# A two-layer hybrid decoder trunk on one core: the first k tile of x^T is multiplied with the first three weight blocks ahead of the second k tile

## The chip, the core and the metric

The kernel runs on one core of a Trainium2 chip. The metric is device time in microseconds (us) of one execution; lower is better. A core has a matrix engine (TensorE, PE in the profile; its weight loads are the row PEld), VectorE (DVE), ScalarE (ACT), GpSimd (POOL) and SyncE (SP), which here only issues transfers (DMAs) to the core's 16 DMA engines. Each engine works through its own instructions in order and waits at semaphores for the others.

## What is computed

Two layers, each with an RMS norm, one wide input projection, four groups of heads, a gate for each group, an output projection and a residual, and a last RMS norm:

```
def hybrid_layer(x, layer_idx, norm_g, w_in, ..., w_out, rope_diff, rope_moba):
    h = rms_norm(x, norm_g)
    p = split_columns(jnp.einsum("bsd,de->bse", h, w_in))
    ...
    mixed = jnp.concatenate([fox, diff, moba, gla], axis=-1)
    return x + jnp.einsum("bse,ed->bsd", mixed, w_out)
```

x is 256 x 2048 in fp32 and w_in has 2048 rows for each layer. Only the start of the first layer's input projection matters in what follows.

## The kernel before

**Three products for one.** The projections are done in a reduced form of fp32 (fp32r), and every operand is split into a high and a low part: `hi` is the operand rounded to fp32r, and `lo` the rest. A product takes three matmuls, high times high, low of x times high of the weights, and high of x times low of the weights. ScalarE makes the high part of the weights (`hi_of`, line 730), VectorE the low part (`lo_of`, line 733). Both are bound to a helper that records each operation, so nearly all instructions show line 466 in the profile, and one goes by the tiles' names.

**x^T.** The transposed x stands ready in memory (`in_xt`) and is loaded into tiles `four`, four k tiles of 128 rows to a tile. `xt_hi` (line 1561) scales a k tile with the norm's weights (`ngt`) into the high half of `hTp`, and `xt_lo` (line 1568) makes the low half on VectorE. The high half is made on VectorE for k tile 0 and on ScalarE for all others. The norm's row factor comes later, from the squares of x^T, and is applied to the results.

**Blocks and steps.** The columns of w_in are cut into blocks. A step is one block with two k tiles (four for a narrow block): one load into a tile `raw` (of which there are 5), a split into `hi` and `lo` (4 of each), then 12 matmuls, since x has two halves of 128 rows (m = 0, 1), 2 k tiles and 3 products. The results of a block add up in PSUM in `mm` tiles or, for the third block, in a `side` tile. In each layer the first three blocks, here A (348 columns), B (512) and C (348), take turns: A, B, C with k tiles 0 and 1, then with k tiles 2 and 3, and so on.

**The first three steps** (`HALVED = 3`) are loaded and split by halves, one k tile each. A0 is block A with k tile 0, A1 with k tile 1, and likewise B0, B1, C0 and C1. The transfers of SyncE are issued by `load` (line 1540), in the order A0, x^T tile 0, A1, x^T tile 1, B0, B1, x^T tiles 2 and 3, C0, C1. The splits are written by `parts_of` (line 1609), step by step: both halves of A with the two x^T tiles, then both halves of B, then of C. `multiply` (line 1812) sorts the products of such a step by half, so TensorE has A0, A1, B0, B1, C0, C1.

**What sets the order of the rest.** A planner in the program (`fill`, `choose`, `split_for`) keeps a rough clock of its own and places each later split and transfer by it when the program is built. A new load into a `raw` tile waits until the split of the step that had the tile is done. The order on each engine is fixed in the built program.

Before the first weights arrive, TensorE multiplies constants (`keep_warm`, line 665).

Of the kernel before, what the change touches and what calls it, by code (L numbers as in the profile page):

```python
# [21 lines left out]
P = 128  # L22
# [15 lines left out]
HALVED = 3  # L38
# [332 lines left out]
def hybrid_trunk(  # L371
# [17 lines left out]
    nc = tc.nc  # L389
    times = Times()  # L390
    cur = {"task": None}

    def give(op):
        if cur["task"] is None:
            emit(op)
        else:
            cur["task"].fifo.append(op)
# [70 lines left out]
    def given_out(key):  # L468
        give(Op("do", lambda: ready.__setitem__(key, times.last)))
# [30 lines left out]
    def fill():  # L500

        for z in list(added):
            if z[0] <= times.now + SOON:
                added.remove(z)
                z[1]()
        load_more()
        busy = True
        while busy:
            busy = False
            passive()  # L510
            for kind in "av":
                e = engines[kind]
                while e.tail < times.now + HORIZON and choose(kind, e):
                    busy = True
                    passive()
# [51 lines left out]
    def matmul(out, lhsT, rhs, start, stop, tiles=1, main=False, **kw):  # L567
        n = int(np.prod(rhs.shape[1:]))
        us = (n * 4 if lhsT.dtype == F32 else n + 32) / 2400.0 / tiles
        give(Op("t", partial(t_.matmul, out, lhsT, rhs, start=start, stop=stop, **kw), [rhs] if main else [lhsT, rhs],  # L570
                [] if main else [out], us))
        if main:
            times.end(out, times.now, "t")
# [156 lines left out]
    def hi_of(hi, src, scale=1.0):  # L730
        a_.activation(hi, src, AF.Copy, scale=scale)

    def lo_of(lo, src, hi):
        v_.tensor_sub(lo, src, hi.bitcast(F32))
# [741 lines left out]
    plan = []  # L1476
# [5 lines left out]
        b = blocks[z["block"]]  # L1482
        plan.append({**z, "block": b, "need": {(b["need"], b["l"], k // 4) for k in z["kts"]}})

    xts = []
    ys = xs.rearrange("p m d -> p (m d)").rearrange("p (c j n) -> p c j n", c=4, j=2)
    mTf = [t.rearrange("p k s -> p (k s)").rearrange("p (f k s) -> p f k s", f=4, k=8) for t in mT]
    orders, ys_to_load, y_free, y_at = [], deque(), {}, {}
# [7 lines left out]
    loads = {"next": 0, "out": 0, "freed": deque(), "at": 0, "left": 0.0, "open": 0}  # L1496

    def load_x(eng, a, b):
        if a % 4 == 0:
            xts.append(s4.get([P, 4, SEQ]))  # L1500
        eng.dma_start(xts[a // 4][:, a % 4:(b - 1) % 4 + 1], xt[:, a:b])
# [38 lines left out]
    def load(i):  # L1540
        s = plan[i]
        if i == 0:
            nc.scalar.dma_start(ngt, norm_gt)
        if i < 24 and i % 6 == 0 and i:
            load_x(nc.sync, i // 6 * 4, i // 6 * 4 + 4)
        per, n = s["block"]["per"], s["block"]["n"]
        raw = wst.tile([P, STEP_W], F32, name="raw", bufs=RAW_BUFS)
        raw = raw[:, :per * n]
        s["raw"] = raw.rearrange("p (j c) -> p j c", j=per)
        src = weights[s["at"]:s["at"] + P * per * n].rearrange("(p c) -> p c", p=P)  # L1550
        if i < HALVED:
            for j in range(2):
                nc.sync.dma_start(raw[:, j * n:(j + 1) * n], src[:, j * n:(j + 1) * n])
                if i == 0:
                    load_x(nc.sync, j, j + 1)
        else:
            q_.move(raw, src, LOADED)
        if i == 1:
            load_x(nc.sync, 2, 4)

    def xt_hi(kt):
        src, g = xts[kt // 4][:, kt % 4], ngt[:, 0, kt:kt + 1]
        if kt == 0:
            v_.tensor_scalar(hT[0][:, kt], src, g, None, op0=OP.mult)
        else:
            hi_of(hT[0][:, kt], src, g)

    def xt_lo(kt):
        v_.scalar_tensor_tensor(hT[1][:, kt], xts[kt // 4][:, kt % 4], ngt[:, 0, kt:kt + 1], hT[0][:, kt].bitcast(F32),
                                op0=OP.mult, op1=OP.subtract)  # L1570

    def split_xt(kts):

        for kt in kts:
            xt_hi(kt)
        for kt in kts:
            xt_lo(kt)
        if kts[-1] % 4 == 3:
            given_out(("h", 0, kts[-1] // 4))
# [29 lines left out]
    def parts_of(s):  # L1609
        per, n = s["block"]["per"], s["block"]["n"]  # L1610
        for name in ("hi", "lo"):
            if s["block"]["kind"] == "apart":
                s[name] = s4.get([P, per, n], F32R)
                continue
            t = wst.tile([P, PART_W], F32R, name=name, bufs=PART_BUFS)
            s[name] = t[:, :per * n].rearrange("p (j c) -> p j c", j=per)
        if not any(s is z for z in plan[:HALVED]):
            s["stages"] = deque([("a", lambda: hi_of(s["hi"], s["raw"]), lambda: times.of(s["raw"])),
                                 ("v", lambda: lo_of(s["lo"], s["raw"], s["hi"]), lambda: times.of(s["hi"]))])
            return  # L1620
        for j in (slice(0, 1), slice(1, 2)):
            hi_of(s["hi"][:, j], s["raw"][:, j])
            if s is plan[0]:
                split_xt((j.start,))
            lo_of(s["lo"][:, j], s["raw"][:, j], s["hi"][:, j])
        loads["freed"].append(times.of(s["lo"]))

    def sum_forms(l):

# [116 lines left out]
    def open_parts(i):  # L1746
        (form_parts if "pair" in plan[i] else parts_of)(plan[i])
# [64 lines left out]
    def multiply(s):  # L1812
        b = s["block"]
        n, (lh, ll) = b["n"], b["lhs"]
        ps = b["ps"]
        if b["kind"] == "apart":
            b.setdefault("steps", []).append(s)
            if s["last"]:
                b["ps1"] = side.get([P, 1024])
            for m, o, steps in ((0, ps[0], [s]), (1, b.get("ps1"), b["steps"])):  # L1820
                if m == 1 and not s["last"]:
                    break
                for z in steps:
                    for j, kt in enumerate(z["kts"]):
                        first, last = z["first"] and j == 0, z["last"] and j == len(z["kts"]) - 1
                        hi, lo, ts = z["hi"][:, j], z["lo"][:, j], slice(m * P, (m + 1) * P)
                        matmul(o[:, :n], lh[:, kt, ts], hi, first, False, main=True)
                        matmul(o[:, :n], lh[:, kt, ts], lo, False, False, main=True)
                        matmul(o[:, :n], ll[:, kt, ts], hi, False, last, main=True)
            return  # L1830
        order = list(enumerate(s["kts"]))
        end = s["last"], len(order) - 1
        products = [(x, part, j, kt) for x, part in ((lh, "hi"), (ll, "hi"), (lh, "lo")) for j, kt in order]
        if any(s is z for z in plan[:HALVED]):
            products.sort(key=lambda z: z[2])
        products = [(*z, m) for z in products for m in range(2)]
        if (s["first"] or s["last"]) and not any(s is z for z in plan[:HALVED]):
            products.sort(key=lambda z: z[4])
        for k, (x, part, j, kt, m) in enumerate(products):
            if k and k % 6 == 0:  # L1840
                loads["left"] = lasts(s) * (1 - k / len(products))
                fill()
            matmul(ps[m][:, :n], x[:, kt, m * P:(m + 1) * P], s[part][:, j],
                   s["first"] and j == 0 and x is lh and part == "hi", part == "lo" and (True, j) == end, main=True)
# [32 lines left out]
    def take_bank(keep=True):  # L1877
        k = banks["next"].popleft()
        if keep:
            banks["next"].append(k)  # L1880
        settle(waiting, k)
        return k, mm.tile([P, 512], F32, name=f"mm{k}", bufs=1)

    def lasts(z):
        return 1.36 if "pair" in z else len(z["kts"]) * (z["block"]["n"] + 32) / 400.0
# [7 lines left out]
    for i in range(ahead):  # L1893
        prepare(i)
        parts_of(plan[i])
        plan[i]["stages"] = ()
# [10 lines left out]
    for i, s in enumerate(plan):  # L1907
# [10 lines left out]
        if i in x_at:  # L1918
            l, k = x_at[i]
            c = slice(k * 512, k * 512 + 512)  # L1920
            src = kept.rearrange("p (m d) -> p m d", m=2)[:, :, c] if l else x[0, :, c].rearrange("(m p) c -> p m c", p=P)
# [5 lines left out]
        if "pair" in s:  # L1927
            if s["form"] == FORM_ORDER[0] and s["first"]:
                k, ps = take_bank(False)
# [58 lines left out]
```

## Time and profile before

| | |
|---|---|
| median of 3 runs | 893.13 us (893.09, 893.13, 894.57) |
| the profiled execution | 892.94 us |
| its span, first to last instruction | 891.2 us |
| TensorE busy | 881.5 us, 99% of the span |
| VectorE, ScalarE busy | 662.2 us, 559.1 us |
| mean granted TensorE clock | 0.998 |
| moved by DMA | 227.45 MB, 255 GB/s in the mean |

A row of the timeline gives the start, the length, the engine, the line, the operation with its output and inputs, their shapes, a count where like instructions follow each other, and in brackets the idle time ahead of it and what ended that. ACTq and SPq are the instruction queues of ScalarE and SyncE, where DMAs are issued. In the list of DMAs the last figure of a row is the time from issue to landing. The chain of waits is followed back from the last instruction of the stretch that was asked for.

### The profile page before, as it was taken

Reading aid. Unit: us, or ns where it says so; the run is one execution under the profiler, and the core shown is the slowest. Engines: PE = TensorE matmul, PEld = TensorE weight load, DVE = VectorE, ACT = ScalarE, POOL = GpSimd, SP = SyncE. Lnnn points to the kernel's source line nnn. Section 1 sums busy time; section 2 is a strip of 40 time slices with the busy share of each in tenths; the row PEclk is TensorE's granted clock in tenths of the full one; section 3 lists DMA queues with packets and bytes.
Section 4 is the critical chain, followed back from the end, with each engine's and each line's share of the span. In section 5 each row is a group of like instructions: output and inputs, shape, how many; then the busy total and the mean of one; then the engine's idle time right before and its main releaser. Section 6 shows DMA issues by size and latency. Waiting matters only on the chain.

```text
span 891.2 us, 12456 instructions
## 1 busy us (share of the span) xinstructions
PE 881.5 (99%) x4380; PEld 750.8 (84%) x4380; DVE 662.2 (74%) x943; ACT 559.1 (63%) x846; POOL 60.0 (7%) x87
## 2 busy tenths in 40 slices
PE   9999999999999999999999999999999999999996
PEld 7988889888887888888899888898888888888886
DVE  6689878878867967656679778879676788585583
ACT  7577675577646667644756876578644575693461
POOL 1010110000110000000000100110000100101000
PEclk9999999999999999999999999999999999999999
DMA  8889897747988685977798898878958978499742
GB/s 289 294 263 303 266 301 241 254 147 263 288 240 274 203 317 178 362 265 228 235 302 265 285 320 224 253 227 277 337 147 262 301 220 271 168 301 363 236 143 96
DMA packets 84142, 227.45 MB, mean 255 GB/s; under 512 B 9979, under 2 KB 30443, under 8 KB 83950
## 3 DMA queue, kind: packets, MB, share of 16 engines
q1 hardware_dynamic: 73336, 192.00, 63.9%
q0 software_dynamic: 9152, 33.03, 14.5%
q10 hardware_dynamic: 1590, 1.62, 0.5%
q8 instruction: 34, 0.56, 0.3%
q14 instruction: 30, 0.25, 0.1%
HBM read 204.06 MB, written 22.55 MB: 254 GB/s over the span
## 4 chain that ended last, share of the span: by engine, by line
PE 93%; DVE 2%; DMA 2%; issue 1%; ACT 1%; SPq 0%; POOLq 0%; POOL 0%; DVEq 0%; ACTq 0%
PE mm L466 79%; PE side L466 14%; DMA raw<-in_weights 2%; DVE lo L466 1%; DVE four L466 1%; ACT hi L466 1%; DMA far<-four 0%; DVE mTl L466 0%; ACT four L466 0%; ACT L466 0%; DVE raw L466 0%; DVE eight L466 0%; SPq L466 0%; POOLq L1984 0%; POOL rf L466 0%
## 5 line engine op out<-in xcount | busy, mean ns | idle before, releaser
L466 ACT ACTIVATE hi<-raw 128x1024 fp32r<-128x1024 f32 (+2 forms) x319 | 316.6, 1011 | 190.9 <-PE mm L466 110.2
L466 PE MATMUL mm<-hi,hTp 128*128 128x512 f32 (+1 forms) x1760 | 432.7, 381 | 1.2 <-ACT hTp L466 0.9
L466 DVE TENSOR_TENSOR lo<-raw,hi 128x1024 fp32r<-128x1024 f32 (+2 forms) x319 | 363.7, 1157 | 93.3 <-ACT hi L466 89.0
L466 PEld LDWEIGHTS mm<-hi,hTp 128*128 128x128 f32 x1760 | 321.5, 188 | 60.3 <-ACT hi L466 1.3
L466 PE MATMUL mm<-lo,hTp 128*128 128x512 f32 (+1 forms) x880 | 237.4, 380 | 0.1
L466 PEld LDWEIGHTS mm<-lo,hTp 128*128 128x128 f32 x880 | 162.4, 188 | 30.6 <-DVE lo L466 0.8
L466 PE MATMUL mm<-hi,mTh 128*128 128x512 f32 (+1 forms) x256 | 69.3, 377 | 0.0
L466 PE MATMUL mm<-lo,mTh 128*128 128x512 f32 (+1 forms) x256 | 69.0, 376 | 0.1
L466 PE MATMUL mm<-hi,mTl 128*128 128x512 f32 (+1 forms) x256 | 69.0, 376 | 0.0
L466 PEld LDWEIGHTS mm<-lo,mTh 128*128 128x128 f32 x256 | 46.2, 188 | 9.2 <-DVE lo L466 0.5
L466 PEld LDWEIGHTS mm<-hi,mTl 128*128 128x128 f32 x256 | 46.3, 188 | 8.8
L466 PEld LDWEIGHTS mm<-hi,mTh 128*128 128x128 f32 x256 | 46.0, 188 | 8.6 <-ACT hi L466 0.4
L466 ACT ACTIVATE four<-mm,rstd 128x512 f32<-128x512 f32 (+2 forms) x56 | 36.7, 667 | 26.3 <-PE mm L466 26.3
L466 POOL DMA_DIRECT2D four<-far x40 | 21.8, 546 | 444.0 <-DMA far<-four 193.5
L466 DVE STREAM_TRANSPOSE four<-four 128x1024 f32<-128x1024 f32 (+1 forms) x34 | 39.1, 1149 | 6.7 <-ACT four L466 6.3
L466 ACT ACTIVATE four<-four 128x512 fp32r<-128x512 f32 (+3 forms) x44 | 35.5, 819 | 12.6 <-DMA four<-far 8.8
L466 PEld LDWEIGHTS side<-four,four 128*128 128x128 f32 (+1 forms) x336 | 37.7, 190 | 3.9 <-issue 1.8
L466 PE MATMUL side<-four,four 128*128 128x128 f32 (+3 forms) x336 | 39.3, 281 | 0.0
L1686 POOL DMA_DIRECT2D xs<-in_weights x24 | 21.2, 900 | 169.5 <-DVE lo L466 36.2
L466 DVE TENSOR_TENSOR lo<-xs,hi 128x1024 fp32r<-128x1024 f32 x24 | 29.1, 1214 | 1.8 <-ACT hi L466 1.8
L466 ACT ACTIVATE mTh<-four 128x1024 fp32r<-128x1024 f32 x16 | 16.9, 1057 | 21.2 <-DVE four L466 21.1
L466 ACT ACTIVATE hi<-xs 128x1024 fp32r<-128x1024 f32 x24 | 25.4, 1060 | 7.1 <-PE mm L466 6.2
(146 smaller groups left out, 685.1 us busy)
## 6 DMA issues: line engine op xcount, KB each, us to landing
raw<-in_weights SPq DMA_DIRECT2D x271, 512.0 KB, 4.9
four<-far POOLq DMA_DIRECT2D x34, 512.0 KB, 6.7
far<-four SPq DMA_DIRECT2D x128, 128.0 KB, 3.9
raw<-in_weights SPq DMA_DIRECT2D x46, 348.0 KB, 5.1
xs<-in_weights POOLq DMA_DIRECT2D x24, 512.0 KB, 8.5
xs<-in_weights SPq DMA_DIRECT2D x8, 512.0 KB, 8.3
xs<-in_x SPq DMA_DIRECT2D x4, 512.0 KB
kept<-xs SPq DMA_DIRECT2D x1, 2048.0 KB, 10.6
```

Of the source, the lines that this page charges most:

```text
L466: op.do()
L1686: g_.eng.dma_start(ys[:, c], weights[at:at + P * 1024].rearrange("(p j c) -> p j c", p=P, j=2), accum_op=OP.add)
```

## The change

The first three steps are still loaded, split and multiplied by halves, but the outer loop now runs over the halves: all of A0, B0, C0 stands ahead of A1, B1, C1, in the transfers, in the splits and in the matmuls. The high part of x^T's k tile 1 is made by VectorE, as that of k tile 0 is. x^T tiles 2 and 3 are loaded after the six halves. The rest of the program is the same but for the planner's order in the steps that follow at once; from the fourth group of x^T's k tiles on, all engines have the same order in both.

```diff
     def load(i):
 ...
         if i < HALVED:
-            for j in range(2):
-                nc.sync.dma_start(raw[:, j * n:(j + 1) * n], src[:, j * n:(j + 1) * n])
-                if i == 0:
-                    load_x(nc.sync, j, j + 1)
+            firsts.append((raw, src, n))
+            if i + 1 == HALVED:
+                for j in range(2):
+                    for k, (to, part, m) in enumerate(firsts):
+                        nc.sync.dma_start(to[:, j * m:(j + 1) * m], part[:, j * m:(j + 1) * m])
+                        if not k:
+                            load_x(nc.sync, j, j + 1)
+                load_x(nc.sync, 2, 4)
         else:
             q_.move(raw, src, LOADED)
-        if i == 1:
-            load_x(nc.sync, 2, 4)
 
     def xt_hi(kt):
         src, g = xts[kt // 4][:, kt % 4], ngt[:, 0, kt:kt + 1]
-        if kt == 0:
+        if kt < 2:
             v_.tensor_scalar(hT[0][:, kt], src, g, None, op0=OP.mult)
         else:
             hi_of(hT[0][:, kt], src, g)
 ...
-        for j in (slice(0, 1), slice(1, 2)):
-            hi_of(s["hi"][:, j], s["raw"][:, j])
-            if s is plan[0]:
-                split_xt((j.start,))
-            lo_of(s["lo"][:, j], s["raw"][:, j], s["hi"][:, j])
-        loads["freed"].append(times.of(s["lo"]))
+        if s is plan[HALVED - 1]:
+            for j in range(2):
+                for z in plan[:HALVED]:
+                    hi_of(z["hi"][:, j], z["raw"][:, j])
+                    if z is plan[0]:
+                        split_xt((j,))
+                    lo_of(z["lo"][:, j], z["raw"][:, j], z["hi"][:, j])
+            loads["freed"].extend(times.of(z["lo"]) for z in plan[:HALVED])
 ...
         if any(s is z for z in plan[:HALVED]):
-            products.sort(key=lambda z: z[2])
+            if s is plan[HALVED - 1]:
+                for j in range(2):
+                    for z in plan[:HALVED]:
+                        for x, part in ((lh, "hi"), (ll, "hi"), (lh, "lo")):
+                            for m in range(2):
+                                matmul(z["block"]["ps"][m][:, :z["block"]["n"]], x[:, z["kts"][j], m * P:(m + 1) * P], z[part][:, j],
+                                       j == 0 and x is lh and part == "hi", False, main=True)
+            return
         products = [(*z, m) for z in products for m in range(2)]
-        if (s["first"] or s["last"]) and not any(s is z for z in plan[:HALVED]):
+        if s["first"] or s["last"]:
             products.sort(key=lambda z: z[4])
```

On SyncE, the first transfers of the program before (a row is the line, the transfer's target and source and the target's shape; 128x348 is a half of A or C, 128x512 from `in_weights` a half of B, `four` a tile of x^T):

```order
L1553 DMA raw<-in_weights 128x348
L1501 DMA four_118<-in_xt 128x256
L1553 DMA raw<-in_weights 128x348
L1501 DMA four_118<-in_xt 128x256
L1553 DMA raw<-in_weights 128x512 x2
L1501 DMA four_118<-in_xt 128x512
L1553 DMA raw<-in_weights 128x348 x2
L466 DMA raw<-in_weights 128x696
```

And in the changed program:

```order
L1556 DMA raw<-in_weights 128x348
L1501 DMA four_120<-in_xt 128x256
L1556 DMA raw<-in_weights 128x512
L1556 DMA raw<-in_weights 128x348 x2
L1501 DMA four_120<-in_xt 128x256
L1556 DMA raw<-in_weights 128x512
L1556 DMA raw<-in_weights 128x348
L1501 DMA four_120<-in_xt 128x512
L466 DMA raw<-in_weights 128x696
```

B0 has moved from the fifth place to the third and C0 from the eighth to the fourth; A1 has moved from the third to the fifth, x^T's tile 1 from the fourth to the sixth, and x^T's tiles 2 and 3 from the seventh to the ninth.

On TensorE, the place behind A0, whose last two matmuls are the first two rows (`mm_165` and `mm_166` are A's results for the two halves of the rows, `mm_179` and `mm_180` B's, `side_181` C's); the rows with a + stand there in the changed program, and the last two rows begin A1:

```order
 L466 MATMUL mm_165<-lo,hTp 128x348
 L466 MATMUL mm_166<-lo,hTp 128x348
+L466 MATMUL mm_179<-hi,hTp 128x512
+L466 MATMUL mm_180<-hi,hTp 128x512
+L466 MATMUL mm_179<-hi,hTp 128x512
+L466 MATMUL mm_180<-hi,hTp 128x512
+L466 MATMUL mm_179<-lo,hTp 128x512
+L466 MATMUL mm_180<-lo,hTp 128x512
+L466 MATMUL side_181<-hi,hTp 128x348 x4
+L466 MATMUL side_181<-lo,hTp 128x348 x2
 L466 MATMUL mm_165<-hi,hTp 128x348
 L466 MATMUL mm_166<-hi,hTp 128x348
```

The six matmuls of B0 and the six of C0 have come between A0 and A1; B1 and C1 follow A1.

On VectorE, the splits of the first steps before (TENSOR_SCALAR is a high part of x^T, SCALAR_TENSOR_TENSOR a low part of it, TENSOR_TENSOR `lo<-raw,hi` a low part of the weights):

```order
L466 TENSOR_SCALAR hTp<-four_118,ngt 128x256
L466 SCALAR_TENSOR_TENSOR hTp<-four_118,ngt,hTp 128x256
L466 TENSOR_TENSOR lo<-raw,hi 128x348
L466 SCALAR_TENSOR_TENSOR hTp<-four_118,ngt,hTp 128x256
L466 TENSOR_TENSOR lo<-raw,hi 128x348
L466 TENSOR_TENSOR lo<-raw,hi 128x512 x2
L466 TENSOR_TENSOR lo<-raw,hi 128x348 x2
```

And in the changed program:

```order
L466 TENSOR_SCALAR hTp<-four_120,ngt 128x256
L466 SCALAR_TENSOR_TENSOR hTp<-four_120,ngt,hTp 128x256
L466 TENSOR_TENSOR lo<-raw,hi 128x348
L466 TENSOR_TENSOR lo<-raw,hi 128x512
L466 TENSOR_TENSOR lo<-raw,hi 128x348
L466 TENSOR_SCALAR hTp<-four_120,ngt 128x256
L466 SCALAR_TENSOR_TENSOR hTp<-four_120,ngt,hTp 128x256
L466 TENSOR_TENSOR lo<-raw,hi 128x348
L466 TENSOR_TENSOR lo<-raw,hi 128x512
L466 TENSOR_TENSOR lo<-raw,hi 128x348
```

The low parts of B0 and C0 now stand ahead of k tile 1 of x^T, whose high part is new on this engine. On ScalarE the high parts of the weights have the same new order, and that of x^T's k tile 1 is gone.

More of the change, by code (lines that the diff above doesn't have):

```diff
@@ L1483, in hybrid_trunk @@
         plan.append({**z, "block": b, "need": {(b["need"], b["l"], k // 4) for k in z["kts"]}})
-    xts = []
+    xts, firsts = [], []
     ys = xs.rearrange("p m d -> p (m d)").rearrange("p (c j n) -> p c j n", c=4, j=2)
```

## The prediction

> **What bounds the kernel now.** I read the busy times first, then who waited for whom on TensorE over the whole span, then the chain of waits and the timeline of the first 13 us, where all of the change lies.
>
> ```profile
> span 891.2 us, 12456 instructions
> PE 881.5 (99%) x4380; PEld 750.8 (84%) x4380; DVE 662.2 (74%) x943; ACT 559.1 (63%) x846; POOL 60.0 (7%) x87
> PE mm L466 <- ACT hTp L466: 0.9, 1, 0.9
> PE side L668 <- PEq L1977: 0.8, 1, 0.8
> PE mm L466 <- DVE hTp L466: 0.2, 1, 0.2
> L466 ACT ACTIVATE hi<-raw 128x1024 fp32r<-128x1024 f32 (+2 forms) x319 | 316.6, 1011 | 190.9 <-PE mm L466 110.2
> ```
>
> TensorE is busy 881.5 of 891.2 us, and its three recorded waits all lie ahead of 7 us. Later it is the others that wait: most of ScalarE's idle time ahead of the `hi` splits is ended by TensorE, which gives buffers back. So time won at the start should travel through to the end, and nothing that the change leaves alone can be won. A busy TensorE still hides short stalls, because ends of matmuls are modelled; I therefore go by starts and by pace.
>
> ```profile
> 4.32 1.01 PE L466 MATMUL mm<-hi,hTp 128*128 128x348 f32 x4 [0.19 <-DVE hTp L466]
> 5.18 0.58 PE L466 MATMUL mm<-lo,hTp 128*128 128x348 f32 x2
> 6.70 1.11 PE L466 MATMUL mm<-hi,hTp 128*128 128x348 f32 x4 [0.94 <-ACT hTp L466]
> 8.08 1.08 PE L466 MATMUL mm<-hi,hTp 128*128 128x512 f32 x4
> 12.76 1.44 PE L466 MATMUL mm<-hi,hTp 128*128 128x348 f32 x8
> ...
> 32.33 1.41 PE L466 MATMUL mm<-hi,hTp 128*128 128x348 f32 x8
> 34.21 1.41 PE L466 MATMUL mm<-hi,hTp 128*128 128x348 f32 x8
> 36.09 2.00 PE L466 MATMUL mm<-hi,hTp 128*128 128x512 f32 x8
> 38.83 1.98 PE L466 MATMUL mm<-hi,hTp 128*128 128x512 f32 x8
> ```
>
> Call the three blocks A (348 columns), B (512), C (348), and their halves A0 (first k tile), A1 (second), and so on. Fed without a gap, 12 matmuls of 348 columns take 34.21 - 32.33 = 1.88 us, and 12 of 512 take 38.83 - 36.09 = 2.74 us. A half is six matmuls: 0.94 us for A or C, 1.37 us for B. The six halves are 6.50 us of work, and they stand from 4.32 to 12.76, which is 8.44 us. **So 1.94 us is all there is to win.** It splits by the starts: A0 has 2.38 us for 0.94 of work (1.44 lost), A1 has 1.38 us for 0.94 (0.44 lost), and B and C together 4.68 us for 4.62 (0.06 lost).
>
> The chain of waits says what A1 waits for:
>
> ```profile
> 1.67 4.04 DMA raw<-in_weights
> 5.73 0.36 ACT hi L466
> 6.14 0.52 ACT hTp L466
> 6.70 4.30 PE mm L466 x18
> ```
>
> The load of A1 is issued at 1.67 and lands at 5.71; then ScalarE makes A1's high part and the high part of x^T's second k tile, one after the other, and VectorE follows with the low ones.
>
> **The change, part by part.** *Ahead of the second half.* The two first loads (A0, x^T tile 0) keep their places, and A0's matmuls still start at 4.32. The next thing that TensorE needs is now B0, which takes the third place on the queue of SyncE. It needs no new x^T, hence one ScalarE operation less than A1 had in its chain, but it is 256 KB where A1 was 174 KB.
>
> ```profile
> core 0: us, PE busy (x) PEld busy (x) DVE busy (x) ACT busy (x) POOL busy (x), PEclk, DMA share, GB/s
> 3.00:4.25 1.25, 1.14 (x4) 0.16 (x2) 0.39 (x2) 0.49 (x1) 0.64 (x3) 1.00 0.73 144
> 4.25:6.25 2.00, 1.44 (x6) 0.92 (x6) 0.88 (x2) 0.52 (x2) 0.00 (x0) 1.00 1.00 340
> 7.50:13.00 5.50, 5.50 (x30) 4.86 (x30) 3.97 (x8) 4.18 (x8) 0.00 (x0) 1.00 1.01 396
> 0.74 0.40 SPq L1553 DMA_DIRECT2D raw<-in_weights  x1
> 4.03 0.91 SPq L1553 DMA_DIRECT2D raw<-in_weights  x2
> 3.37 0.49 ACT L466 ACTIVATE hi<-raw 128x348 fp32r<-128x348 f32 x1 [0.67 <-DMA raw<-in_weights]
> 6.72 1.30 ACT L466 ACTIVATE hi<-raw 128x512 fp32r<-128x512 f32 x2
> 9.34 0.96 ACT L466 ACTIVATE hi<-raw 128x348 fp32r<-128x348 f32 x2 [1.32 <-DMA raw<-in_weights]
> ```
>
> A landing of B0 stands in no row, since its load was fourth or later. The 82 KB more than A1 (84,000 bytes) cost 0.58 us at the 144 GB/s of 3.00 to 4.25, or 0.25 us at the 340 GB/s right after. I take 0.25, since the slow stretch had ended 1.5 us ahead of A1's landing: B0 lands at 5.71 + 0.25 = 5.96. From below the bound is 4.3, which is 1.67 plus the 2.63 us that A0 took (issued at 0.74, ScalarE starts at 3.37); from above 7.0, which is 1.67 plus the 5.3 us of the slowest of these halves (C0: issued at 4.03, ScalarE starts at 9.34).
>
> ScalarE takes 1.30 us for two 512-column splits, 0.65 for one, so with about 0.04 us of handover TensorE starts B0 at 6.65. That is only 0.05 us ahead of the 6.70 of A1: **the wait stays and changes its name**, from ACT hTp to ACT hi.
>
> *Behind it.* From 6.65 there are 5.56 us of work (6.50 less A0). If nothing is late, the six halves end at 12.21, or 12.27 with the 0.06 us that B and C lose now. The second block step for A then starts at 12.27, where it started at 12.76: **0.49 us earlier**, most of it the 0.44 us that A1 loses today. What could be late:
>
> ```profile
> 3.83 0.35 DVE L466 TENSOR_SCALAR hTp<-four,ngt 128x256 fp32r<-128x256 f32 x1 [2.89 <-DMA four<-in_xt]
> 6.68 0.48 DVE L466 SCALAR_TENSOR_TENSOR hTp<-four,ngt,hTp 128x256 fp32r<-128x256 f32 x1 [1.56 <-ACT hTp L466]
> L466 DVE TENSOR_TENSOR lo<-raw,hi 128x348 fp32r<-128x348 f32 x4 | 2.0, 518 | 1.1 <-ACT hi L466 1.1
> L466 DVE TENSOR_TENSOR lo<-raw,hi 128x512 fp32r<-128x512 f32 x2 | 1.3, 688 | 0.0
> four<-in_xt SPq DMA_DIRECT2D x1, 128.0 KB, 3.9
> ```
>
> VectorE gets the second k tile's high part (0.35 us, as for the first) and stands to it after B's and C's low parts. With whole durations from 6.65: B0 lo to 7.34, C0 lo to 7.86, high part to 8.21, low part to 8.69, A1 lo to 9.21. TensorE reaches A1 at 6.65 + 1.37 + 0.94 = 8.96, needs x^T's low part two matmuls later at 9.27 and A1's low part at 9.59. The tightest margin is 0.38 us, so the moved split costs nothing. Without that cover, each 0.1 us of it would cost 0.1 us. Its x^T tile is now sixth on SyncE, about 3.1 us (the places stand 0.47 us apart, from 0.74 for the first to 1.67 for the third), and lands at 7.0 by the 3.9 us of the row above, in time for 7.86. ScalarE loses that operation (0.45 us of its pace), which only eases it.
>
> B1 and C1 stay behind the same bytes within 174 KB. C0 landed at 9.33 as eighth of the nine loads. B1 is now seventh, and even at 9.33 its high part would be ready at 9.98, against TensorE at 9.90 (0.08 us lost); as seventh it should come earlier. C1 needs its high part by 11.27 only. x^T's tiles 2 and 3 become the last of the nine:
>
> ```profile
> 10.21 0.89 ACT L466 ACTIVATE hTp<-four,ngt 128x256 fp32r<-128x256 f32 x2
> 11.01 0.77 ACT L466 ACTIVATE hi<-raw 128x696 fp32r<-128x696 f32 x1
> 12.65 1.04 ACT L466 ACTIVATE hi<-raw 128x1024 fp32r<-128x1024 f32 x1
> 14.17 0.91 ACT L466 ACTIVATE hTp<-four,ngt 128x256 fp32r<-128x256 f32 x2 [0.47 <-DMA four<-in_xt]
> SPq L466 <- DVE lo L466: 1.6, 1, 1.6
> 7.68 0.33 SPq L466 DMA_DIRECT2D raw<-in_weights  x1
> ```
>
> All nine were there before 10.21, as ScalarE took C0, C1 and these tiles without a wait after 9.34. Even with today's times the next step's high part is ready at 11.78 and the following one's at 13.69, where TensorE would want them at 12.27 and 14.15. Both hold, the second by 0.46 us.
>
> *A buffer freed later.* The sixth raw load has to wait for A's buffer. It was issued at 7.68, after VectorE's low part of A1; this comes to 9.21 now, so that load, x^T's tiles 4 to 7 behind it and the next raw loads go out some 1.5 us later. I cost that at nothing: the two loads ahead (348 and 512 KB) are 2.2 us of the 396 GB/s at which the DMA engines run without a gap from 7.50 to 13.00, so the late ones join a queue that is not yet empty. Bounds: 0, or 1.5 us on the landing of x^T's tiles 4 to 7, 14.17 then 15.7. Their user on TensorE starts at 19.33 today and 18.84 then, with some 2.6 us of splitting between, so even the upper end is hidden.
>
> *Sum.* 0.49 us off the profiled execution of 892.94 us (span 891.2 and 1.74 around it) gives 892.45. The median shown, 893.13, is 0.19 above that execution, so **the forecast for a median is 892.6 us**, 0.05% faster. A measurement of this kernel tells about 0.2% from no change, 1.8 us, so this counts as the same.
>
> **A rule beside the rows.** The trace gives A0 2.63 us from issue to use and A1 4.04, for the same 174 KB. The Trainium skill, page "DMA: Bandwidth & Descriptors", section "Anatomy of one DMA — SWDGE (gpsimd) path", puts one transfer at some 2.0 us plus its bytes over 436 GB/s, fitted on the other kind of queue; A1 would be 2.4 us by it, so the trace does not bear it out here. By it B0 would land at 4.3, and the sum would be that of the first rival.
>
> **Rivals.**
> 1. *The third load lands as fast as the first.* If A1 was late for its own sake and not for its place, B0 lands at 4.3 (the lower bound), and TensorE goes from A0 to B0 with no wait but A0's own one for its low part (last matmul started about 5.34, so B0 at 5.5). The end of the halves is 5.5 + 5.56 + 0.06 = 11.1: 1.64 us won, 891.5 as a median. For it speaks A0's 2.63 us; against it that the x^T tile behind A1 took 3.9 too. 15%.
> 2. *B0 is the slower one*, the case on the other side. Every 0.1 us that B0 lands behind 5.96 takes 0.1 us from the gain. From a landing at 6.45 on the change loses; at the upper bound, 7.0, B0 starts at 7.69 and the result is 0.55 us slower, 893.7. For it speaks the 144 GB/s of 3.00 to 4.25, if that belongs to the third load rather than to the time (then 6.3, and 0.15 us won); against it the 340 GB/s right behind. 20%.
> 3. *Nothing arrives at the end*: a later stretch is set by loads and swallows the 0.49 us, 893.1. For it speaks that the kernel's DMA engines are near their rate early on; against it that TensorE has no recorded wait after 7 us. 5%.
> 4. *The late buffer reaches TensorE.* x^T's tiles 4 to 7 decide from a landing at about 17.5 on, 3.3 us later than today; a landing at 20 would cost 2 us net and give over 895. For it speaks the 1.5 us; against it the queue above. 5%.
>
> **How the numbers follow.** 55% for the forecast (0.2 to 0.9 us won), then 15, 20, 5 and 5. The range takes in the first two rivals, 891.5 to 893.7, and 0.4 us above for runs that scatter upwards (one of the three stands at 894.57): 891.5 to 894.1. Faster by over 0.2% needs nearly the whole 1.94 us: 3%. Slower by over 0.2% is the fourth rival or something unseen: 5%. The rest, 92%, lies within.
>
> **What would show it.** In the profile after: TensorE's one wait of 0.9 us near 6 us now on ACT hi, ended by a 512-column split; B0's matmuls at about 6.65; C0 and A1 without idle time between; the step that stood at 12.76 near 12.27; x^T's second high part on VectorE near 8; tiles 4 to 7 of x^T still used near 14 to 15. The first wait shorter than 0.3 us would mean rival 1, one above 1.3 us rival 2, and an idle TensorE between 17 and 20 us rival 4. A start near 12.27 with an unchanged total would mean rival 3.

## The result

| | before | changed |
|---|---|---|
| median of 6 runs each | 893.35 us (893.09 to 894.57) | 897.75 us (896.77 to 901.24) |
| ratio | 1 | 1.0057, 95% interval 1.0036 to 1.0078 |
| the profiled execution | 892.94 us | 896.77 us |
| its span | 891.2 us | 895.0 us |

The change makes the kernel 0.57% slower, some 4.4 us, where the forecast was 892.6 us and the range ended at 894.1. In the experiments further down, one execution of e6 took 1487 us at a mean granted clock of 0.556; it is left out of that kernel's ratio, though not out of its median. The totals of the engines hardly moved, but TensorE's waits did:

```profile
span 895.0 us, 12453 instructions
PE 882.8 (99%) x4380; PEld 750.8 (84%) x4380; DVE 662.2 (74%) x944; ACT 558.6 (62%) x845; POOL 60.1 (7%) x87
PE mm L466 <- DVE lo L466: 1.4, 3, 0.9
PE mm L466 <- ACT hi L466: 1.3, 2, 0.8
PE side L466 <- DVE lo L466: 0.3, 1, 0.3
```

In the list of waits (engine, tile, line, what it waited for; then total us, times, longest) the wait on ACT hTp is gone. In its place stand six others, 3.0 us in all: the one that was forecast (0.46 us, below) and five that weren't. The question is where in the span they lie.

**The first 13 us** are won. The timeline of TensorE after:

```profile
4.16 1.02 PE L466 MATMUL mm<-hi,hTp 128*128 128x348 f32 x4
6.05 1.20 PE L466 MATMUL mm<-hi,hTp 128*128 128x512 f32 x4 [0.46 <-ACT hi L466]
8.50 0.81 PE L466 MATMUL mm<-hi,hTp 128*128 128x348 f32 x4
11.90 1.54 PE L466 MATMUL mm<-hi,hTp 128*128 128x348 f32 x8
```

B0 starts at 6.05, A1 follows B0 and C0 with no wait at 8.50, and the next step starts at 11.90 instead of 12.76. To see what becomes of the 0.86 us, I take the same matmul in both traces and subtract its start before from its start after; this **lag** is negative while the changed kernel leads. Each entry is the middle one of seven neighbouring rows of TensorE's timeline, at the place that before reaches at the time in the heading (us). The kernels e1 to e12 are those of the experiments; each row is one profiled execution, so small steps of one kernel are not yet a rule.

| | 13 | 22 | 45 | 56 | 200 | 515 | 530 | 885 |
|---|---|---|---|---|---|---|---|---|
| changed | -0.77 | 0.31 | 0.32 | 1.56 | 1.57 | 1.53 | 3.10 | 3.17 |
| e8, changed again | -0.75 | 0.93 | 0.95 | 3.20 | 3.21 | 3.20 | 4.19 | 4.17 |
| e1, planner's look | -0.79 | -0.79 | -0.78 | 3.68 | 3.75 | 3.70 | 4.24 | 4.22 |
| e2, high part on ScalarE | 0.24 | 0.71 | 0.75 | 6.77 | 7.14 | 7.08 | 7.40 | 7.90 |
| e3, small loads on GpSimd | -0.55 | 0.75 | 0.76 | 0.76 | 0.82 | 0.76 | 0.34 | 0.32 |
| e5, e1 and e3 together | -0.48 | -0.47 | -0.47 | -0.48 | 0.56 | 0.60 | 0.94 | 0.91 |
| e9, e1 with A1 third | -0.92 | -0.94 | -0.94 | -0.95 | -0.24 | -0.24 | 1.30 | 1.64 |
| e4, before, small loads on GpSimd | -0.24 | -0.26 | -0.26 | -0.26 | 0.62 | 0.59 | 1.66 | 1.63 |
| e6, before, A's buffer held | -0.59 | 0.52 | 0.53 | 1.50 | 1.46 | 1.43 | 3.46 | 3.67 |
| e7, e6 with small loads on GpSimd | -0.09 | 0.46 | 0.46 | 0.46 | 1.11 | 1.07 | 2.28 | 2.26 |

The changed kernel loses in three places: 1.1 us from 13 to 22, 1.2 us from 45 to 56, and 1.6 us from 515 to 530. The span grew by 3.8 us, 0.6 more than the last lag; that rest lies behind the last matmul and isn't followed here.

**First loss, 16 to 21 us.** VectorE and TensorE in the timeline after, and of before the one row that differs:

```profile
15.06 0.88 DVE L466 SCALAR_TENSOR_TENSOR hTp<-four,ngt,hTp 128x256 fp32r<-128x256 f32 x2
16.70 0.89 DVE L466 SCALAR_TENSOR_TENSOR hTp<-four,ngt,hTp 128x256 fp32r<-128x256 f32 x2 [0.75 <-ACT hTp L466]
17.51 0.88 DVE L466 TENSOR_TENSOR lo<-raw,hi 128x696 fp32r<-128x696 f32 x1
18.44 0.89 PE L466 MATMUL side<-lo,hTp 128*128 128x348 f32 x4 [0.35 <-DVE lo L466]
20.80 0.89 PE L466 MATMUL mm<-lo,hTp 128*128 128x348 f32 x4 [0.21 <-DVE lo L466]
```

```profile
15.79 1.68 DVE L466 TENSOR_TENSOR lo<-raw,hi 128x696 fp32r<-128x696 f32 x2
```

All four low parts of x^T's tile stand ahead of the sixth step's low part now, which starts at 17.51; before it started at 15.79, between the two pairs. The changed `multiply` records all 36 matmuls of the three steps without the `fill()` that came after every six, so the planner finds fewer moments at which to place splits. (e6 and e7 lose time here too, with the planner's old order. That is another path, told with those runs.)

**Second loss, 46 to 50 us.** Here the chain of waits after tells the whole path:

```profile
38.08 7.35 DMA xs<-in_weights
...
45.46 0.24 ACTq L466
...
45.75 1.07 ACT four L466
...
48.37 0.89 DVE lo L466
...
49.30 1.55 PE mm L466 x8
```

ScalarE's queue stands still. From 38 us on it issues a constant and the six small loads of `in_gla_wa` and `in_gla_ba` (`constants`, lines 676 to 681), and in the built program each of the last five carries a wait of its own:

```
L466 DMA four_508<-in_gla_wa 16x2x256 [waits Pool_49]
L466 DMA four_508<-in_gla_ba 1x512 [waits DMAHW5_49]
L466 DMA four_508<-in_gla_wa 16x2x256 [waits DMAHW6_49]
L466 DMA four_508<-in_gla_ba 1x512 [waits DMAHW7_49]
L466 DMA four_508<-in_gla_wa 16x2x256 [waits DMAHW0_49]
L466 DMA four_508<-in_gla_ba 1x512 [waits DMAHW1_49]
```

The program names its DMA semaphores DMAHW0 to DMAHW7 and hands them out again, so a transfer waits until an earlier one with the same semaphore has landed, here transfers of SyncE. By the chain of waits the last of the six waited for the `xs` load, issued at 38.08. ScalarE's next operation, and the high parts behind it, wait for all of that. The row of this operation before, then after:

```profile
42.97 1.06 ACT L466 ACTIVATE four<-four 128x1024 f32<-128x1024 f32 x1 [3.26 <-DMA four<-in_gla_wa]
```

```profile
45.75 1.06 ACT L466 ACTIVATE four<-four 128x1024 f32<-128x1024 f32 x1 [5.72 <-DMA four<-in_gla_wa]
49.30 0.59 PE L466 MATMUL mm<-lo,hTp 128*128 128x348 f32 x2 [0.86 <-DVE lo L466]
```

The bracket says DMA four<-in_gla_wa, the nearest transfer; the chain and the program's waits show that the weight loads were behind it. Before, ScalarE's 3.26 us cost TensorE nothing; behind the 5.72 us TensorE waits 0.86. The Trainium skill, page "DMA: Bandwidth & Descriptors", section "Anatomy of one DMA — SWDGE (gpsimd) path", says that DMA engines do not wait at semaphores, and that such a wait is served on the sequencer that issues the transfer. The row agrees: it is ScalarE that stands still.

Why do these loads land later? SyncE's queue before and after (start, length from the first to the last issue, count):

```profile
4.98 3.03 SPq L466 DMA_DIRECT2D raw<-in_weights  x3
8.05 0.43 SPq L1501 DMA_DIRECT2D four<-in_xt  x1
17.87 0.42 SPq L1501 DMA_DIRECT2D four<-in_xt  x1
28.10 0.43 SPq L1501 DMA_DIRECT2D four<-in_xt  x1
```

```profile
4.98 3.75 SPq L466 DMA_DIRECT2D raw<-in_weights  x3
8.77 0.43 SPq L1501 DMA_DIRECT2D four<-in_xt  x1
21.19 0.43 SPq L1501 DMA_DIRECT2D four<-in_xt  x1
30.87 0.42 SPq L1501 DMA_DIRECT2D four<-in_xt  x1
```

The sixth raw load is issued 0.72 us later (4.98 + 3.75 against 4.98 + 3.03 for its end), since A's buffer comes free later; x^T's third and fourth tile groups are 3.3 and 2.8 us later. That these lag so much more is in part the planner's order: in e1, which has the late buffer but not that order, the third group is issued at 19.34, 1.5 us later than before. The stretch from 16 to 24 us shows what that did to the DMA engines; the last two figures are their busy share and GB/s, before, then changed:

```profile
16.00:24.00 8.00, 8.00 (x47) 7.55 (x47) 7.34 (x9) 5.74 (x9) 0.00 (x0) 1.00 0.91 285
```

```profile
16.00:24.00 8.00, 7.44 (x43) 6.67 (x42) 6.77 (x8) 5.38 (x8) 0.00 (x0) 1.00 0.69 201
```

The engines ran partly dry, 84 GB/s over 8 us or 0.67 MB behind. Not all of that is the late buffer: with the old order on VectorE the same stretch has 275 GB/s in e1 and 261 in e6, both with A's buffer late, and 300 in e9, where it is free earlier. So the deep dip is mostly the planner's order. From 4 to 38 us the rate is 308 to 316 GB/s in before, e4 and e12, 290 to 311 in the five with the late buffer and the old order (e1, e5, e6, e7, e11), and 283 to 289 in the changed kernel, e2, e3 and e8; the means are 313, 298 and 286. By these means a little over half of what is missing at 38 us is the late buffer's, an estimate, since single profiles scatter.

The missing bytes are made up in front of the `xs` load: issued only 0.31 us later than before (38.08 against 37.77), it took 7.35 us. From 4 us to the issue of the last small load, before (42.68) and after (45.46):

```profile
4.00:42.68 38.68, 37.55 (x201) 33.60 (x201) 28.55 (x43) 25.01 (x39) 0.00 (x0) 1.00 0.94 317
```

```profile
4.00:45.46 41.46, 40.43 (x216) 36.18 (x216) 28.61 (x44) 24.50 (x38) 0.00 (x0) 1.00 0.88 298
```

That is 12.3 and 12.4 MB. In e1, e2, e6, e8 and e9, where the last small load is issued between 42.92 and 48.17 us, it is 12.4 to 12.5 MB. In all seven profiles ScalarE gets past the small loads when about the same number of bytes has come, however early it reached them.

**Third loss, 515 to 530 us.** Nothing of the program differs there. In the chain after, a weight load takes 12.37 us, and ScalarE waits for it:

```profile
511.37 12.37 DMA raw<-in_weights
```

```profile
524.95 1.19 PE L466 MATMUL mm<-hi,hTp 128*128 128x512 f32 x4 [0.85 <-ACT hi L466]
```

The lags show the same place in kernels whose start is that of before: e4 loses 1.1 us there, e6 2.0, while e3, which keeps the change, gains 0.4. And it differs between executions of one program: e12, which is e4 again, loses nothing there (0.82 on both sides). So this loss isn't tied to the change.

### The profile page after: what moved, and what is told of

Same layout as the page of the kernel before. It is cut to its first block, busy times and chain, and to the rows that moved or that the text cites. A ratio compares the mean times of both kernels' runs of the same rounds, so it can differ in the third digit from the quotient of the medians.

```text
span 895.0 us, 12453 instructions
## 1 busy us (share of the span) xinstructions
PE 882.8 (99%) x4380; PEld 750.8 (84%) x4380; DVE 662.2 (74%) x944; ACT 558.6 (62%) x845; POOL 60.1 (7%) x87
## 4 chain that ended last, share of the span: by engine, by line
PE 90%; DMA 4%; DVE 3%; ACT 2%; issue 1%; SPq 0%; DVEq 0%; POOLq 0%; POOL 0%; ACTq 0%
PE mm L466 77%; PE side L466 13%; DMA raw<-in_weights 2%; DVE lo L466 1%; ACT hi L466 1%; DVE four L466 1%; DMA xs<-in_weights 1%; DMA four<-in_xt 1%; ACT four L466 0%; DMA far<-four 0%; DVE mTl L466 0%; ACT hTp L466 0%; SPq L466 0%; ACT L466 0%; DVE raw L466 0%
```

## The experiments

Three sets of four kernels ran, each with runs of the kernel before on the same chip; in these, before scattered from 892.3 to 901.3 us, so only medians of several runs and ratios are read as times.

**e1: the planner's look between the half steps.** The changed kernel, with `fill()` called ahead of each half step but the first:

```diff
-                    for z in plan[:HALVED]:
+                    for k, z in enumerate(plan[:HALVED]):
+                        if j or k:
+                            loads["left"] = (6 - 3 * j - k) * 0.92
+                            fill()
```

> The changed kernel, with the planner asked to place splits and loads after each half again (as before it was asked every six matmuls), which brings the order on VectorE behind the first steps back to nearly that of before: two low parts of x^T, the fifth step's low part, two more low parts of x^T. Theory A (the loss of 4.4 us comes from that order: a late low part of the fifth step keeps its buffer, the loads behind it go out up to 3 us later, and two later places of the program run out of data): the loss goes and the 0.86 us won on the first six halves stays, 892.5 us, 891.5 to 893.3. Rival B (the new order of loads, or the halves themselves, cost it whatever the planner does): 897 to 898 us.

Measured 896.01 us, ratio 1.0014 (1.0002 to 1.0026), between what theory A and rival B expected. The first loss is gone: the lag stays at -0.79 until 45 us, so the missing looks were its cause. But a larger loss comes at 46 to 50 us:

```profile
46.31 1.06 ACT L466 ACTIVATE four<-four 128x1024 f32<-128x1024 f32 x1 [7.38 <-DMA four<-in_gla_wa]
```

```profile
48.09 0.90 PE L466 MATMUL mm<-hi,hTp 128*128 128x348 f32 x4 [1.52 <-ACT hi L466]
49.86 0.69 PE L466 MATMUL mm<-lo,hTp 128*128 128x348 f32 x2 [0.86 <-DVE lo L466]
```

All engines come to the small loads earlier and find the weight loads no earlier. What was won at the start is waited away here, and more.

**e2: the high part back on ScalarE.**

```diff
-        if kt < 2:
+        if kt == 0:
```

> The changed kernel with the high part of x^T's second k tile made by ScalarE, as before; the planner's order still has four low parts of x^T ahead of the fifth step's low part. Theory A: no better than the changed kernel, 897 to 899 us. Rival C (the operation added to VectorE pushes everything behind it there): most of the 4.4 us comes back, 893 to 894 us.

Measured 901.07 us, ratio 1.0072 (1.0060 to 1.0084), slower than either side expected. Inside the change the move to VectorE helps: without it the lag is 0.24 instead of -0.77 at 13 us, and the loss behind 45 us is the largest of all, 6.0 us. The move doesn't cause the slowdown.

**e3 and e4: the six small loads issued by GpSimd**, in the changed kernel and in the one before; the rest of the order is untouched.

```diff
         for i in range(0, 96, 32):
-            a_.move(w3[i:i + 16], gla_wa2.rearrange("l r e -> r l e"), CONSTANT)
-            a_.move(w3[i + 16:i + 17]...
+            give(Op("da", partial(g_.eng.dma_start, w3[i:i + 16], gla_wa2.rearrange("l r e -> r l e")), ...
+            give(Op("da", partial(g_.eng.dma_start, w3[i + 16:i + 17]...
```

> The changed kernel with six small loads (weights and bias of the gate's second projection, some 100 KB) issued by GpSimd in place of ScalarE; the order on every engine is otherwise the same. In the changed kernel ScalarE is idle for 5.7 us around 43 us, since it issues these loads in between and each waits for an earlier weight load to land. Theory A: the wait at 46 to 50 us goes, 1.3 us, 896.4 us, and if the later loss of 1.5 us near 524 us hangs on the first one, 894.9 us. Rival D (ScalarE's wait is not what TensorE waits for at 49 us): 897 to 898 us.

> Control for the run on the changed kernel: the kernel before, with the same six small loads issued by GpSimd. ScalarE's wait of 3.3 us there is covered, as TensorE has no wait near 46 to 50 us. Theory A: the same within 0.5 us, 892.9 to 893.9 us. Rival E (moving these loads helps by itself, whatever the order of the first steps): 891.5 to 892.5 us.

e3 measured 894.96 us, ratio 0.9998 (0.9984 to 1.0011); e4 893.59 us, ratio 0.9993 (0.9984 to 1.0001). With one edit that touches nothing of the change, the changed kernel is level with before. It is not level with e4, which has the same edit and ran on the same chip: the medians are 1.4 us apart, the means 1.2 us (95% interval 0.4 to 1.8, by resampling the runs). So the small loads are behind most of the slowdown, and something over 1 us is not theirs; the first loss, which e3 keeps (-0.55 to 0.75 in the lags), is of that size. ScalarE's operation is at 41.56 now and waits 1.04 us, for VectorE:

```profile
41.56 1.06 ACT L466 ACTIVATE four<-four 128x1024 f32<-128x1024 f32 x1 [1.04 <-DVE hTp L466]
```

The lag of e3 stays at 0.76 from 22 to 56 us, although its DMA engines were as dry (195 GB/s from 16 to 24 us). So the late loads cost nothing there but by way of ScalarE's queue.

**e5: e1 and e3 together.**

> The changed kernel with both: the planner's look between the half steps, and the six small loads issued by GpSimd. Theory A (two losses, the low parts put ahead on VectorE at 16 to 21 us and ScalarE's queue held by the small loads at 38 to 46 us): the lead of 0.6 to 0.8 us that the look kept until 45 us now lasts past 50 us, no wait of TensorE over 0.5 us between 40 and 55 us, 893.0 to 894.2 us, 0.5 to 1.5 us below before. Rival D (the later weight loads cost time elsewhere as well): 895 or more.

Measured 893.37 us, ratio 0.9983 (0.9969 to 0.9996), 1.0 us under before. The lead lasts past 56 us (-0.48). It is then lost near 86 us, of which below.

**e6 and e7: only the buffer.** The kernel before with one instruction more, which holds A's raw buffer until VectorE has B's second low part; e7 has the small loads on GpSimd besides.

```diff
+    held = cp.tile([P, 1], F32, name="held")
 ...
+        if s is plan[1]:
+            nc.vector.tensor_copy(held, plan[0]["raw"][:, 0, 0:1])
```

> The kernel before with one more instruction on VectorE, a copy of one column of A's raw block behind B's second low part, so that A's buffer comes free about 1 us later and nothing else moves. Theory A: the sixth raw load and the transfers behind it go out 0.5 to 1.2 us later, ScalarE's wait in the small loads grows from 3.3 us to 4 us or more, TensorE waits 0.3 us or more between 46 and 51 us where it waited nothing, and the time is 0.5 to 4 us above before. Rival E (the late buffer is slack; the loss comes from the order of the half steps): no wait at 46 to 51 us, within 0.5 us of before.

> The same, with the six small loads issued by GpSimd. Theory A: the buffer is as late, but nothing of ScalarE stands behind the small loads: no wait at 46 to 51 us, within 0.5 us of before. Rival F (the late buffer costs by itself, through the loads behind it): as late as the kernel with the column held and the small loads on ScalarE.

e6 measured a median of 895.34 us against 894.38, ratio 0.9999 (0.9983 to 1.0016). e7: 894.31 us, ratio 0.9991 (0.9978 to 1.0005). By time e6 isn't told from before. The profile tells more, SyncE first, then ScalarE and TensorE in e6, each at two places:

```profile
4.98 4.67 SPq L466 DMA_DIRECT2D raw<-in_weights  x3
16.13 0.91 ACT L466 ACTIVATE hTp<-four,ngt 128x256 fp32r<-128x256 f32 x2 [2.65 <-DMA four<-in_xt]
17.77 1.54 PE L466 MATMUL side<-hi,hTp 128*128 128x348 f32 x8 [0.75 <-ACT hi L466]
45.69 1.06 ACT L466 ACTIVATE four<-four 128x1024 f32<-128x1024 f32 x1 [5.45 <-DMA four<-in_gla_wa]
49.25 0.59 PE L466 MATMUL mm<-lo,hTp 128*128 128x348 f32 x2 [0.72 <-DVE lo L466]
```

The load is 1.64 us later (4.67 against 3.03), more than expected; near 46 us ScalarE waits 5.45 us and TensorE 0.72, at the same place and on the same tiles as in the changed kernel, and the lag rises by 0.97 from 45 to 56 us. In e7 it doesn't move there (0.46 and 0.46). The late buffer is enough for a second loss without any of the other edits, if a smaller one than in the changed kernel.

The two rows in between are a cost that was not expected: x^T's tiles 4 to 7 reach ScalarE at 16.13 instead of 14.17, the sixth step's high part stands behind them on ScalarE, and TensorE waits 0.75 us for it. From 13 to 22 us the lag rises by 1.1 in e6 and 0.55 in e7. In the changed kernel, with a delay of 0.72 us, those tiles are in use at 14.52 and nothing waits for them.

**e8: the changed kernel again.**

> The changed kernel once more, on the chip of these runs. Both theories: 3 to 6 us above before, and a wait of TensorE at 46 to 50 us behind ScalarE's high part; theory A adds that this wait is 0.5 to 2.5 us and differs between executions, with a lower granted clock behind it where it is longest.

Measured 899.04 us against 894.38, ratio 1.0048 (1.0032 to 1.0064). The profiled execution waits 0.86 us on ScalarE's high part at 49.17 and 0.86 on VectorE's low part at 50.94, 2.25 us of lag, where the first profile had a single wait of 0.86 and 1.24 us of lag. The wait differs between executions, as expected; the clock stayed at 1.00 in this one.

**e9 and e10: A's buffer early, the change kept.** As e1, but the halves in another order, in transfers, splits and matmuls alike; e10 has the small loads on GpSimd besides.

```diff
+HALVES = ((0, 0), (0, 1), (1, 0), (0, 2), (1, 1), (1, 2))
 ...
-                for j in range(2):
-                    for k, (to, part, m) in enumerate(firsts):
+                for j, k in HALVES:
+                    to, part, m = firsts[k]
```

> The changed kernel with the planner's look between the half steps, the six small loads on ScalarE as they were, and the half steps in the order A0, B0, A1, C0, B1, C1 (loads, splits and products alike): A's raw block is split, and its buffer free, about as early as before. Theory A: SyncE issues the sixth raw load near 8 us instead of 8.7, the loads behind it go out early, ScalarE's wait in the small loads falls from 7.4 us to about 4, and TensorE waits under 1 us between 46 and 51 us; 892.5 to 895, 1 us or more below the run with the look alone. Rival E (TensorE's lead alone makes ScalarE late at the small loads): the same 2 to 2.5 us of waits as with the look alone, 896 or more.

> The same with the six small loads on GpSimd: no wait over 0.5 us between 12 and 60 us; 892.5 to 894.0, as with the look and the small loads on GpSimd. If later buffers cost anything besides the small loads, this one is faster than that one by more than 0.5 us.

e9 measured 894.31 us, ratio 0.9991 (0.9979 to 1.0002); e10 894.41 us (0.4 over what was expected), ratio 0.9987 (0.9975 to 0.9999). In e9 the small loads are still on ScalarE and TensorE leads by 0.94 us, more than in e1; yet:

```profile
4.99 3.37 SPq L467 DMA_DIRECT2D raw<-in_weights  x3
43.21 1.06 ACT L467 ACTIVATE four<-four 128x1024 f32<-128x1024 f32 x1 [4.45 <-DMA four<-in_gla_wa]
```

The sixth load is 0.6 us earlier than in e1, ScalarE waits 4.45 us instead of 7.38, and TensorE has no wait at all between 12 and 60 us; the lag stays at -0.94. The rival, that the lead alone makes ScalarE late, falls. e10 isn't faster than e9 beyond the intervals, so no loss by the small loads is seen where the weight loads come in time.

**e11 and e12: e5 and e4 side by side.**

> The look and the small loads on GpSimd once more, on the chip of the next run: 893.0 to 894.0. If the won half step (0.6 to 0.8 us) reaches the end, it is 0.3 to 1.0 us below the kernel before with the small loads on GpSimd; if it is lost on the way, the two are within 0.3 us.

> The kernel before with the six small loads on GpSimd, on the same chip: 893.3 to 894.3, with no wait of TensorE between 46 and 51 us, as in its first run.

893.56 us, ratio 0.9981 (0.9970 to 0.9993), and 893.83 us, ratio 0.9988 (0.9976 to 0.9999). Both are faster than before, by 0.19% and 0.12%; between them lie 0.27 us, which by what was written ahead means that the won half step doesn't reach the end, as far as these runs can tell (the means are 0.4 us apart, 95% interval -1.3 to 0.5). In both, TensorE waits 0.34 us near 86 us on VectorE's low part, and the lag there goes from -0.36 to 0.30 and from -0.60 to 0.83. That wait is in e4, e5, e7 and e10 as well, all with the small loads on GpSimd, but not in e3, and the chain of waits in e12 leads to a weight load of 9.47 us:

```profile
66.43 9.47 DMA raw<-in_weights
```

Why it lands so late, here and near 520 us, stays open.

## Why the prediction was wrong

**What held.** The mechanism of the first 12 us is as predicted: the wait changes its name to ACT hi, no half is late behind it, and the high part of x^T moved to VectorE (7.08 us) delays nothing. Only sizes were off. B0 landed at 5.35, not 5.96, as the chain after shows:

```profile
1.66 3.69 DMA raw<-in_weights
```

So the two profiles show 0.86 us won instead of 0.49. But before's profile was on the late side: e4, e6, e7 and e12 start like it and stand at -0.24, -0.59, -0.09 and -0.57 at 13 us, with before's 0 a mean of -0.30; the six executions with the change's start (changed, e8, e1, e3, e5, e11) have a mean of -0.62. By these single profiles the half steps win about 0.3 us, an estimate. The second and third rivals, a slower B0 and a time that comes out unchanged, did not come true, and the first one's landing at 4.3 wasn't reached. But what the third rival feared, a later stretch that is set by loads and swallows the gain, is what e5, e11 and e12 show near 86 us; that time won at the start travels to the end was taken for granted.

**The step that failed** is "A buffer freed later. I cost that at nothing", with its reason that "the late ones join a queue that is not yet empty". The delay of the sixth load was even shorter than the 1.5 us taken (0.72), but the queue did not make it up: from 4 to 38 us the DMA engines ran at 289 GB/s where before ran at 308, and by the means above a little over half of such a gap comes with the late buffer alone. I had looked only at the next user of the data, x^T's tiles 4 to 7, and put a price on it up to 15.7 us. The bill came at 38 to 46 us and to another engine: to ScalarE, whose queue held six small loads waiting for landings of SyncE's. e6 shows this cost with the buffer alone, e9 shows it gone with the buffer earlier, e3 shows it gone with the small loads elsewhere. That chain wasn't among the rivals; the fourth had the late buffer, but at 17 to 20 us. e6 shows that this rival was priced too low as well. It lets x^T's tiles 4 to 7 land as late as 17.5, though 18.84 less the 2.6 us of splitting is 16.2, and it looks at their own products alone. With these tiles in use at 16.13, TensorE already waited 0.75 us at 17.77, for the step before, whose high part stands behind them on ScalarE.

**A second term was left out.** The planner's new order in the next steps was named ahead of the prediction and given no price in it. It cost 1.1 us at 16 to 21 us, more than the half steps had won; e1 brings it back.

**What stays open.** e3 is level with before and some 1.2 us above e4, so around 3 of the 4.4 us hang on the small loads, an estimate. The losses at 46 to 50 us in the changed kernel's two profiles make 1.2 and 2.3 us of it. Of its six executions the two around 901 us had a mean clock of 0.993 against 0.997 to 0.998; e1 and e2 show the half clock behind such a wait, and that this is the rest wasn't shown for the changed kernel itself. How much of the lateness at 38 us is the buffer's and how much the planner's order is only estimated: no run has the new order with the buffer early.

## What to carry to other kernels

When a buffer comes free later, follow every queue that waits for a landing, not only the reader of the next tile: look in the built program for waits of DMA issues on an engine that computes, and compare the DMA engines' share by stretches. A bandwidth that is nearly full early on isn't slack for a late transfer; what it misses is made up in front of later ones. And a small load belongs on an engine that nobody waits for; where ScalarE is held by bytes still to come, as in e1, a lead won upstream is only waited away there.

## What the hardware showed beside this

Behind the longest waits TensorE's granted clock fell. Stretches of e1, e2 and e8 (stretch, its length, then busy times of PE, PEld, DVE, ACT and POOL, and the clock):

```profile
48.00:50.00 2.00, 1.05 (x5) 0.76 (x6) 1.93 (x5) 2.00 (x4) 0.00 (x0) 1.00 0.00 0
50.00:52.00 2.00, 2.00 (x8) 2.00 (x9) 2.00 (x2) 0.61 (x1) 0.00 (x0) 0.54 0.59 184
52.00:54.00 2.00, 2.00 (x9) 1.82 (x9) 0.23 (x2) 0.00 (x0) 0.72 (x2) 0.60 0.93 291
```

```profile
54.00:56.00 2.00, 2.00 (x9) 1.90 (x8) 0.38 (x2) 0.00 (x0) 0.32 (x1) 0.50 0.92 289
```

```profile
50.00:52.00 2.00, 1.14 (x7) 1.06 (x7) 2.00 (x4) 1.69 (x3) 0.00 (x0) 1.00 0.09 18
```

In e1 the clock fell to half behind waits of 1.52 and 0.86 us with matmuls between them; 0.54 and 0.60 in two stretches of 2 us are some 3.4 us at half. In e2 it fell at 50.6 us, behind one wait of 2.14 us that ended at 50.24; the wait of 0.53 us came later, and 0.65, 0.50, 0.50 and 0.64 in the stretches from 50 to 58 us are some 6.8 us at half. Two waits of 0.86 us, 1.72 in all, in e8 left it at 1.00. The Trainium skill, page "TensorE: Matmul & The Clock Gate", section "What's actually happening", puts the fall to half rate behind an idle window of about 3.4 us. Here less than that was enough, 2.14 us in e2; the measurement decides.
